# Inputs of the first stage laid out beforehand, and one column group of TensorE for each modulation tile

## The chip, the cores and the metric

The kernel runs on one core of one Trainium2 chip. The metric is the device time of one execution in microseconds (us). Times are told as the median of several executions; the rows come from one more execution that the hardware profiler recorded.

## The reference, cut to what matters

Two transformer blocks run one behind the other on 512 tokens of 1024 channels, in float32. The change lies in the first stage of the first block, and in two smaller inputs of it:

```python
c_act = jax.nn.silu(c)                                   # c: (1, 1024)
cond = c_act @ ada_w[i] + ada_b[i]                       # ada_w: (1024, 6 * 1024)
shift1, scale1, gate1, shift2, scale2, gate2 = jnp.split(cond, N_MOD, axis=-1)
h = modulate(rmsnorm(x, norm1_g[i]), shift1, scale1)     # h * (1 + scale) + shift
z = h @ w_in[i] + b_in[i]                                # w_in: (1024, 2048)
u, v, val, gate = jnp.split(z, [D_A, 2 * D_A, 2 * D_A + D_B], axis=-1)
...
w = jnp.where(causal[None], w_s, jnp.zeros_like(w_s))    # w_s: (8, 128, 128)
mixed = jnp.einsum('hts,bcshd->bcthd', w, v) + b_s ...
```

The rest is a causal convolution of width 31 on val * sigmoid(gate), an output projection, a gated feed-forward layer, an attention block with three branches, a pooling block and two more feed-forward layers.

## The kernel before, in words

Activations stand with channels on partitions: `Xp` holds x as four tiles of two channel blocks by 512 tokens, `H` holds the modulated h as eight tiles of a high and a low part (`hx.t[k][:, 0]` and `[:, 1]`). Every product of the model is done in three float32r matmuls (high by high, high by low, low by high), so each weight slab that arrives (`raw`, 512 KB) is split by ScalarE into a high part `wh` and by VectorE into a low part `wl`; the class `Weights` (`W`) loads slabs in the planned order and splits them, and `W.ahead(n)` makes sure that n are split.

The first stage runs from the start to the last product of the "wave". Its parts, in the order in which the program gives them:

- `load_vecs` brings small vectors as rows (tile `rows`), and its `turn` transposes them on TensorE into columns. `turn_c` does this for c, `turn_1` for the norm gain and the modulation bias; `turn_2`, `turn_3` and `turn_4` come later.
- x arrives with tokens on partitions (four tiles `xtok`). ScalarE squares each half of a tile and sums it along the way (`accum_out`), a square root and a reciprocal give `rsc`, 32 transposes turn x into `Xp`, and `spread` makes a row of reciprocals on all partitions with four matmuls.
- `piece(q)`, q = 0 to 3, computes two channel blocks of shift1 and two of scale1: `ada_cols` multiplies the 32-fold copy `c32` of silu(c) with two slabs of `ada_w` at a time. Four column groups of 32 columns of the array each take one block of input channels and 256 output columns; the four partial sums are transposed and added by VectorE (`tensor_reduce`).
- `front(q)` makes two tiles of H from `Xp`, the row of reciprocals, and the modulation.
- `products(q)` does 24 matmuls with these two tiles, for four output tiles that stay open over all q (`wave`). With `WV = (6, 0)` and `WT = 4`, 6 products run, then the 16 matmuls of `piece(q + 1)`, then 4 products, then the transposes of the piece, `front(q + 1)`, and the other 14 products.

In this stage the instructions of VectorE, ScalarE and TensorE stand in program order (`ordered(True)`); the DMA queue of SyncE and everything behind the stage is ordered by the compiler's planner. The planner also decides which tile takes which place in SBUF, so a load can wait for the last reader of the tile that stood in its place. A float32 matmul (not float32r) is two instructions of TensorE in the trace.

Behind the wave comes the convolution (taps on VectorE and GpSimd), the v projection, the spatial mixing, whose weights `wsr` are masked by GpSimd and transposed in eight matmuls into `wsT`, and `turn_4`. All helpers issue on one line, so the profile shows L113 for nearly all compute; the tiles tell them apart. L218 is `load_vecs`, L237 loads x, L249 is `ada_load`, L309 is `W.load`.

Of the kernel before, what the change touches and what calls it, by code (L numbers as in the profile page):

```python
# [22 lines left out]
KF0 = 14  # L23
KT0 = 16
LD = 2
WV = (6, 0)
WT = 4
DEEP = 2
DEEPF = 1
# [1 line left out]
HS = 256  # L31
# [50 lines left out]
PS3 = 1  # L82


TAGS = {}
TAGSETS = 0
B1 = ("cv", "glu", "bvs", "wsr", "wsT", "vt", "uT")
NB1 = 11
WW = ()
NBW = 20  # L90
TAGS.update({n: ("b1", NB1) for n in B1})
# [29 lines left out]
def body(ctx: ExitStack, tc: tile.TileContext, I: dict, out, dbg=None):  # L121
    nc = tc.nc
    cp = ctx.enter_context(tc.tile_pool(name="cp", bufs=1))
# [5 lines left out]
    V, G, SC, TE = (Ordered(tc, e) for e in (nc.vector, nc.gpsimd, nc.scalar, nc.tensor))  # L129
# [11 lines left out]
    def SQ():  # L141
        return tp.tile([P, S], F32, tag="sq", name="sq", bufs=BS)
# [27 lines left out]
    def stt(o, a, s, b, op0, op1):  # L170
        return V.scalar_tensor_tensor(o, a, s, b, op0=op0, op1=op1)
# [36 lines left out]
    def flat(apx):
        n = len(apx.shape)
        letters = "abcde"[:n]  # L210
        return apx.rearrange(f"{' '.join(letters)} -> ({' '.join(letters)})") if n > 1 else apx

    def load_vecs(gi, grp, eng=nc.sync):

        rt = rows.rearrange("p a (s c) -> p (a s) c", c=P)[:, gi]
        r0 = 0
        for name, src, n in grp:
            eng.dma_start(rt[r0:r0 + n, :P], flat(src).rearrange("(r p) -> r p", p=P))  # L218
            r0 += n

        def turn():
            pt = ST()
            TE.transpose(pt[:, :r0], rt[:r0, :P], ident[:r0, :r0])
            col = C(r0)
            V.tensor_copy(col, pt[:, :r0])
            c0 = 0
            for name, src, n in grp:
                vecs[name] = col[:, c0:c0 + n]
                c0 += n
        return turn  # L230

    rows = A("rows")
    turn_c = load_vecs(0, [("c", I["c"], 8)])
    xt = []
    for i in range(4):
        a = A("xtok")
        nc.sync.dma_start(a, I["x"][0, i * P:(i + 1) * P, :].rearrange("p (j c) -> p j c", j=2))  # L237
        xt.append(a)
    turn_1 = load_vecs(1, [("norm1", I["norm1_g"], 8), ("adab", I["ada_b"], 48), ("b_in", I["b_in"], 16)], nc.scalar)
# [36 lines left out]
    Xp = [cp.tile([P, 2, S], F32, name=f"X{q}") for q in range(4)]  # L276

    def x_(k, c0=0, c1=S):
        return Xp[k // 2][:, k % 2, c0:c1]

    H = [cp.tile([P, 2, S], F32R, name=f"H{k}") for k in range(KD)]

# [61 lines left out]
    def plan_cols(w, k0, kt, c0, n):  # L344
        W.plan([(0, P, 0, n, rows_of(w, k0, kt, c0, n))], kt, n)

    w_in = I["w_in"][0]
    for c in range(4):
        W.pool = c < WP
        W.hp = HP  # L350
        plan_cols(w_in, 0, 8, 1024 + c * P, P)
        plan_cols(w_in, 0, 8, 1536 + c * P, P)
    for b in range(4):
        plan_cols(w_in, 2 * b, 2, 512, S)
    for c in range(4):
        plan_cols(w_in, 0, 8, c * P, P)
    for k0 in (0, 4):
        for g in range(4):
            plan_cols(I["w_out"][0], k0, 4, g * HS, HS)
# [185 lines left out]

    adaw = []
    for q in range(4):
        if q < 2:
            W.load()
            W.load()  # L550
        adaw.append([ada_load(ada, c0 + HS * q, HS) for c0 in (0, D)])
    turn_2 = load_vecs(2, [("cw", I["b_conv_w"], 124)])
    turn_3 = load_vecs(3, [("norm2", I["norm2_g"], 8), ("normf", I["norm_f_g"], 8), ("conv_b", I["b_conv_b"], 4), ("gn_g", I["b_gn_g"], 4),
                           ("gn_b", I["b_gn_b"], 4), ("ona", I["out_norm_a_g"], 4), ("onb", I["out_norm_b_g"], 4), ("lng", I["a_ln_g"], 4),
                           ("lnb", I["a_ln_b"], 4), ("psc", I["pool_scale_2"], 8), ("adafb", I["ada_f_b"], 16), ("pe", I["nsa_cmp_pe_2"], 32)])

    ordered(True)
    turn_c()
    act(cact, vecs["c"], AF.Silu)
    V.tensor_copy(c32, cact.unsqueeze(2).to_broadcast([P, KD, 32]))  # L560
    ssx = C(8).rearrange("p (a b) -> p a b", a=4)
    rsc = C(4)
    for i in range(4):
        for j in range(2):
            act(SQ(), xt[i][:, j], AF.Square, accum_out=ssx[:, i, j:j + 1])
    V.tensor_reduce(rsc, ssx, axis=AX.X, op=OP.add)
    act(rsc, rsc, AF.Sqrt, scale=1.0 / D, bias=epsc)
    V.reciprocal(rsc, rsc)
    for k in range(KD):
        pt = AXP()  # L570
        for i in range(4):
            TE.transpose(pt[:, i * P:(i + 1) * P], xt[i][:, k // 4, (k % 4) * P:(k % 4 + 1) * P], ident)
        V.tensor_copy(x_(k), pt)
    rsx = ACC()
    act(rsx, spread(rsc, S), AF.Copy)
    W.ahead(2)
    turn_1()
    adab = vecs["adab"]

# [191 lines left out]
    for q in range(4):  # L771
        w = products(q)
        if q < 3:
            pc = piece(q + 1)
            for n in WV:
                for _ in range(n):
                    next(w)
                for _ in range(8):
                    next(pc)
            for _ in range(WT):  # L780
                next(w)
            drain(pc)
            front(q + 1)
# [952 lines left out]
```

## Time and profile before

| | |
|---|---|
| runs | median of 3: 1685.77 us (1684.52 to 1688.46) |
| profiled execution | 1689.51 us, its span 1687.8 us |
| TensorE busy | 1651.7 us, 98% of the span |
| VectorE, ScalarE, GpSimd busy | 857.5, 686.3, 130.1 us |
| granted TensorE clock, mean | 0.991 |

The span runs from the first to the last instruction; 1.7 us of the profiled execution lie outside it. A granted clock of 1.00 is 2.4 GHz and 0.50 is 1.2 GHz. Busy time of TensorE is modelled at its end, so a busy TensorE isn't one at its peak.

### The profile page before, as it was taken

To read this page: it belongs to the slowest core of one execution; us is meant where nothing else is said; L and a number is where in the kernel's file an instruction comes from. 1 tells how busy PE (TensorE), PEld (TensorE's weight loads), DVE (VectorE), ACT (ScalarE), POOL (GpSimd) and SP (SyncE) were. 2 spreads that over 40 slices of the span, in tenths; PEclk is the share of its full clock that TensorE was granted. 3 is DMA by queue.
4 is the path that set the end of the run, shared out by engine and by line. 5 is a ranking of instruction groups with operands and counts; after the bars stand their busy time and mean duration, and the time that the engine had idled before them with its cause. 6 is when DMAs were issued, how large, how long until landed. Compare 5 with 4: busy or idle time off the path is not lost.

```text
span 1687.8 us, 22593 instructions
## 1 busy us (share of the span) xinstructions
PE 1651.7 (98%) x9033; PEld 1370.7 (81%) x9033; DVE 857.5 (51%) x1636; ACT 686.3 (41%) x1246; POOL 130.1 (8%) x144
## 2 busy tenths in 40 slices
PE   7998999999999999999999999999998999999998
PEld 4885798777888998877768988888887998888886
DVE  5798672333333485678776434433248744341244
ACT  4685452232222364446558422223237832222222
POOL 0452000000000002100002000000012100000002
PEclk8998999999999999999999999999999999999999
DMA  9636544455331424311125223234321432232511
GB/s 302 177 117 197 181 114 129 148 165 164 89 103 57 113 61 94 89 38 37 40 72 147 70 80 96 88 113 121 92 87 51 133 98 70 76 114 98 150 38 50
DMA packets 263602, 179.58 MB, mean 106 GB/s; under 512 B 20688, under 2 KB 244800, under 8 KB 263496
## 3 DMA queue, kind: packets, MB, share of 16 engines
q1 hardware_dynamic: 258952, 176.99, 36.0%
q10 hardware_dynamic: 4544, 1.14, 0.4%
q8 instruction: 71, 1.16, 0.3%
q14 instruction: 35, 0.29, 0.1%
HBM read 175.99 MB, written 2.11 MB: 106 GB/s over the span
## 4 chain that ended last, share of the span: by engine, by line
PE 93%; DVE 3%; ACT 2%; DMA 2%; SPq 1%; issue 0%; DVEq 0%; ACTq 0%
PE mm L113 84%; PE ax L113 4%; PE st L113 4%; DMA raw<-in_w_ffn_in_dram 1%; DMA adaw<-in_ada_w_dram 0%; SPq L249 0%; DMA raw<-in_w_out_dram 0%; ACT sq L113 0%; DVE wl L113 0%; ACT pw L113 0%; DVE pw L113 0%; DVE ax L113 0%; DVE XT L113 0%; ACT wh L113 0%; ACT H L113 0%
## 5 line engine op out<-in xcount | busy, mean ns | idle before, releaser
L113 PE MATMUL mm<-H,wh 128*128 128x512 f32 (+1 forms) x3168 | 872.8, 361 | 2.2 <-ACT H L113 2.2
L113 PEld LDWEIGHTS mm<-H,wh 128*128 128x128 f32 x3168 | 563.5, 189 | 99.1 <-issue 9.1
L113 PE MATMUL mm<-H,wl 128*128 128x512 f32 (+1 forms) x1584 | 568.5, 359 | 0.0
L113 DVE TENSOR_TENSOR wl<-raw,wh 128x1024 fp32r<-128x1024 f32 (+1 forms) x257 | 311.8, 1226 | 281.4 <-ACT wh L113 262.7
L113 PEld LDWEIGHTS mm<-H,wl 128*128 128x128 f32 x1584 | 299.9, 189 | 44.4 <-issue 1.0
L113 ACT ACTIVATE wh<-raw 128x1024 fp32r<-128x1024 f32 (+1 forms) x257 | 262.2, 1041 | 146.0 <-PE mm L113 89.5
L113 PE MATMUL mm<-wh,hid 128*128 128x512 f32 x704 | 217.3, 389 | 0.0
L113 DVE TENSOR_TENSOR silu<-silu,mm 128x512 f32<-128x512 f32 (+1 forms) x77 | 47.0, 611 | 256.9 <-PE mm L113 252.9
L113 PEld LDWEIGHTS mm<-wh,hid 128*128 128x128 f32 x704 | 132.1, 188 | 27.2
L113 ACT ACTIVATE hid<-silu 128x512 fp32r<-128x512 f32 (+1 forms) x77 | 43.9, 570 | 268.0 <-DVE silu L113 268.0
L113 PE MATMUL mm<-wl,hid 128*128 128x512 f32 x352 | 137.3, 390 | 0.0
L113 PE MATMUL mm<-hid,wh 128*128 128x512 f32 (+1 forms) x464 | 116.6, 340 | 0.0
L113 PEld LDWEIGHTS mm<-hid,wh 128*128 128x128 f32 x464 | 80.2, 190 | 10.0 <-issue 0.4
L113 POOL TENSOR_TENSOR mg<-mg,gb 128x512 f32<-128x512 f32 x32 | 44.4, 1395 | 467.7 <-ACT sq L113 424.3
L113 ACT ACTIVATE silu<-silu 128x512 f32<-128x512 f32 (+1 forms) x52 | 29.3, 565 | 124.4 <-DVE silu L113 124.3
L113 PE MATMUL mm<-hid,wl 128*128 128x512 f32 (+1 forms) x232 | 79.0, 340 | 0.0
L113 PEld LDWEIGHTS mm<-wl,hid 128*128 128x128 f32 x352 | 66.1, 188 | 14.0 <-DVE wl L113 0.3
L113 DVE TENSOR_TENSOR silu<-mm,rsb 128x512 f32<-128x512 f32 (+1 forms) x52 | 31.6, 608 | 73.7 <-PE mm L113 73.2
L113 DVE TENSOR_TENSOR hid<-silu,hid 128x512 fp32r<-128x512 f32 (+1 forms) x77 | 47.3, 615 | 36.9 <-ACT hid L113 36.8
L113 PE MATMUL mm<-wh,H 128*128 128x512 f32 (+2 forms) x256 | 65.4, 344 | 0.2 <-ACT H L113 0.2
L113 POOL TENSOR_TENSOR cv<-cv,tap 128x488 f32<-128x488 f32 (+12 forms) x40 | 53.5, 1370 | 91.6 <-ACT cv L113 71.3
L113 ACT ACTIVATE silu<-mm 128x512 f32<-128x512 f32 (+1 forms) x25 | 13.6, 546 | 95.4 <-PE mm L113 95.4
(263 smaller groups left out, 1648.5 us busy)
## 6 DMA issues: line engine op xcount, KB each, us to landing
adaw<-in_ada_w_dram SPq DMA_DIRECT2D x48, 512.0 KB
raw<-in_w_ffn_in_dram SPq DMA_DIRECT2D x44, 512.0 KB
raw<-in_ffn_w_gate_dram SPq DMA_DIRECT2D x44, 512.0 KB
raw<-in_ffn_w_up_dram SPq DMA_DIRECT2D x44, 512.0 KB
raw<-in_ffn_w_down_dram SPq DMA_DIRECT2D x44, 512.0 KB
raw<-in_w_in_dram SPq DMA_DIRECT2D x16, 512.0 KB
adaw<-in_ada_f_w_dram SPq DMA_DIRECT2D x16, 512.0 KB
raw<-in_attn_w_in_dram SPq DMA_DIRECT2D x16, 512.0 KB
```

The source lines that it names most:

```text
L113: ins = f(*a, **k)
```

## The change

x, the vectors, the modulation weights of the first two parts, the input projection and the spatial weights are put in other orders of the same numbers before the launch (`laid_out`), so that each partition reads one contiguous run: 4 KB for x, for a slab of modulation weights, for a slab of w_in and for the spatial weights. In the kernel the transposes of x, of the vectors and of the spatial weights are gone. The sums of squares of x, which now run across partitions, are made by TensorE: for each of eight channel blocks ScalarE squares the block and four float32 matmuls with a column of ones add it up. In `piece`, a column group of 32 columns now computes one of the four 128-wide output blocks over all eight channel blocks, so nothing is left to add behind it; it is 32 matmuls of 128 columns in place of 16 of 256, one transpose in place of four. The modulation weights of q = 0 are loaded ahead of the first two weight slabs, and the split of these slabs moves from ahead of `piece(0)` into `front(0)`. `WV` becomes (20, 8, 8): the number of products ahead of the piece, for each q.

```diff
-WV = (6, 0)
+WV = (20, 8, 8)
-B1 = ("cv", "glu", "bvs", "wsr", "wsT", "vt", "uT")
-NB1 = 11
+B1 = ("cv", "glu", "bvs", "wsT", "vt", "uT")
+NB1 = 10
...
-    rows = A("rows")
-    turn_c = load_vecs(0, [("c", I["c"], 8)])
-    xt = []
-    for i in range(4):
-        a = A("xtok")
-        nc.sync.dma_start(a, I["x"][0, i * P:(i + 1) * P, :].rearrange("p (j c) -> p j c", j=2))
-        xt.append(a)
-    turn_1 = load_vecs(1, [("norm1", ...), ("adab", ...), ("b_in", ...)], nc.scalar)
+    def load_vecs(src, names, eng):
+        n = sum(w for _, w in names)
+        col = C(n)
+        eng.dma_start(col, I[src])
+        c0 = 0
+        for name, w in names:
+            vecs[name] = col[:, c0:c0 + w]
+            c0 += w
...
+    load_vecs("va", VA, nc.scalar)
+    for q in range(4):
+        nc.sync.dma_start(Xp[q], I["xt"][q])
...
+    def plan_win(c):
+        W.plan([(0, P, 0, P, I["w_in_p"][c].rearrange("p (k m) -> p k m", k=8))], 8, P)
...
     for q in range(4):
+        sl = [A("adaw") for _ in range(4)]
+        for a, src in zip(sl, I["ada_p"][q]):
+            nc.sync.dma_start(a, src)
+        adaw.append(sl)
         if q < 2:
             W.load()
             W.load()
-        adaw.append([ada_load(ada, c0 + HS * q, HS) for c0 in (0, D)])
-    turn_2 = load_vecs(2, ...)
-    turn_3 = load_vecs(3, ...)
+    load_vecs("vb", VB, nc.sync)
...
-    for i in range(4):
-        for j in range(2):
-            act(SQ(), xt[i][:, j], AF.Square, accum_out=ssx[:, i, j:j + 1])
-    V.tensor_reduce(rsc, ssx, axis=AX.X, op=OP.add)
-    act(rsc, rsc, AF.Sqrt, scale=1.0 / D, bias=epsc)
+    pst = ST()
+    for k in range(KD):
+        q = SQ()
+        act(q, x_(k), AF.Square)
+        for i in range(4):
+            TE.matmul(pst[:, i:i + 1], lhsT=q[:, i * P:(i + 1) * P], rhs=ones[:, 0:1], start=(k == 0 and i == 0), stop=(k == KD - 1 and i == 3))
+    act(rsc, pst[:, :4], AF.Sqrt, scale=1.0 / D, bias=epsc)
     V.reciprocal(rsc, rsc)
-    for k in range(KD):
-        pt = AXP()
-        for i in range(4):
-            TE.transpose(pt[:, i * P:(i + 1) * P], xt[i][:, k // 4, (k % 4) * P:(k % 4 + 1) * P], ident)
-        V.tensor_copy(x_(k), pt)
-    rsx = ACC()
-    act(rsx, spread(rsc, S), AF.Copy)
-    W.ahead(2)
-    turn_1()
+    rsp = spread(rsc, S)
+    rsx = ACC()
...
     def piece(q):
-        g = [ada_cols(adaw[q][x], 8 * x + 2 * q, adab[...], AXP) for x in range(2)]
...
+        pq = AXP()
+        for k in range(KD):
+            for j in range(4):
+                yield TE.matmul(pq[32 * j:32 * j + 32, :P], lhsT=c32[:, k, :], rhs=adaw[q][k // 2][:, k % 2, j * P:(j + 1) * P],
+                                start=(k == 0), stop=(k == KD - 1))
+        sb = T("adasb")
+        act(sb[:, :P], pq[:, :P], AF.Copy)
+        pt = AXP()
+        yield TE.transpose(pt[:, :P], sb[:, :P], ident)
+        for x in range(2):
+            ks = slice(8 * x + 2 * q, 8 * x + 2 * q + 2)
+            tt(mod[:, ks], pt[:, :P].rearrange("p (j r) -> p j r", j=4)[:, 2 * x:2 * x + 2, 0], adab[:, ks], OP.add)
...
-    def front(q):
+    def front(q, rs, between=None):
...
-                stt(t, x_(k), g1[:, k:k + 1], rsx, OP.mult, OP.mult)
+                stt(t, x_(k), g1[:, k:k + 1], rs, OP.mult, OP.mult)
...
+            if k == 2 * q + 1 and between is not None:
+                between()
...
-    front(0)
+    front(0, rsp, lambda: W.ahead(2))
+    act(rsx, rsp, AF.Copy)
...
-            for n in WV:
-                for _ in range(n):
-                    next(w)
-                for _ in range(8):
-                    next(pc)
+            for _ in range(WV[q]):
+                next(w)
+            for _ in range(32):
+                next(pc)
...
-    turn_2()
-    turn_3()
...
-    wsr = A("wsr")
     wsT = A("wsT")
-    nc.sync.dma_start(wsr.rearrange(...), I["a_spatial_w"][0].rearrange("h t s -> t h s"))
-    G.affine_select(wsr, wsr, pattern=[[0, 8], [-1, P]], ...)
-    turn_4 = load_vecs(4, [("ng2", I["norm_g_2"], 64)])
+    nc.sync.dma_start(wsT, I["wst"])
+    G.affine_select(wsT, wsT, pattern=[[0, 8], [1, P]], ...)
...
-    for b in range(2):
-        pt = ST()
-        for h in range(4):
-            TE.transpose(pt[:, h * P:(h + 1) * P], wsr[:, b, h * P:(h + 1) * P], ident)
-        act(wsT[:, b], pt, AF.Copy)
-    turn_4()
...
+def laid_out(a):
+    import numpy as np
+    a = {k: np.asarray(v) for k, v in a.items()}
+    for name, group in (("va", VA), ("vb", VB)):
+        a[name] = np.concatenate([a[SOURCE[v]].reshape(w, P).T for v, w in group], axis=1)
+    a["xt"] = a["x"][0].T.reshape(4, 2, P, S).transpose(0, 2, 1, 3)
+    p = a["ada_w"][0][:, :2 * D].reshape(4, 2, P, 2, 4, 2, P)
+    a["ada_p"] = p.transpose(4, 0, 2, 1, 3, 5, 6).reshape(4, 4, P, 2, S)
+    a["w_in_p"] = a["w_in"][0].reshape(KD, P, 16, P).transpose(2, 1, 0, 3).reshape(16, P, D)
+    a["wst"] = a["a_spatial_w"][0].transpose(2, 0, 1).reshape(P, 2, S)
+    return a
```

The loads of the w_in slabs for val, gate and u go through `plan_win`; the four slabs for v stay as they were. `VA` and `VB` list the vectors with their numbers of columns: 80 columns for c, the norm gain, the modulation bias and the input bias, 288 for the others.

## Rows read from the trace of the kernel before

**Rows 1.** The page: the chain that ended last, share of the span by engine.

```profile
PE 93%; DVE 3%; ACT 2%; DMA 2%; SPq 1%; issue 0%; DVEq 0%; ACTq 0%
```

**Rows 2.** Timeline of TensorE, first stage: start, us taken, operation, count, [idle before].

```profile
19.24 0.96 PE L113 MATMUL ax<-adaw,fixed 128*32 128x256 f32 x8 [0.85 <-DMA adaw<-in_ada_w_dram]
...
23.62 1.58 PE L113 MATMUL mm<-H,wh 128*128 128x512 f32 x2 [2.19 <-ACT H L113]
...
26.84 3.30 PE L113 MATMUL ax<-adaw,fixed 128*32 128x256 f32 x32
...
36.21 1.93 PE L113 MATMUL ax<-adaw,fixed 128*32 128x256 f32 x32
```

**Rows 3.** The chain that ended last, in order of time: start, us.

```profile
47.70 8.65 PE mm L113 x38
```

**Rows 4.** Timeline of ScalarE, first stage.

```profile
4.92 0.63 ACT L113 ACTIVATE sq<-xtok 128x512 f32<-128x512 f32 x1 [1.19 <-DMA xtok<-in_x_dram]
...
12.32 0.30 ACT L113 ACTIVATE fixed<-fixed 128x4 f32<-128x4 f32 x1
...
15.93 1.99 ACT L113 ACTIVATE wh<-raw 128x1024 fp32r<-128x1024 f32 x2
...
20.31 0.38 ACT L113 ACTIVATE adasb<-ax 128x256 f32<-128x256 f32 x1 [2.11 <-PE ax L113]
...
22.85 1.39 ACT L113 ACTIVATE H<-t,fixed 128x512 fp32r<-128x512 f32 x2 [2.16 <-DVE t L113]
```

**Rows 5.** Timeline of VectorE, first stage and around 136 us.

```profile
12.65 0.18 DVE L113 RECIPROCAL fixed<-fixed 128x4 f32<-128x4 f32 x1 [1.45 <-ACT fixed L113]
...
17.51 2.35 DVE L113 TENSOR_TENSOR wl<-raw,wh 128x1024 fp32r<-128x1024 f32 x2
...
23.60 1.41 DVE L113 SCALAR_TENSOR_TENSOR H<-t,fixed,H 128x512 fp32r<-128x512 f32 x2
...
136.69 1.22 DVE L113 TENSOR_TENSOR wl<-raw,wh 128x1024 fp32r<-128x1024 f32 x1 [1.39 <-ACT wh L113]
```

**Rows 6.** Timeline of SyncE's DMA queue: issue time, time taken, load, count.

```profile
0.80 0.40 SPq L218 DMA_DIRECT2D rows<-in_c_dram  x1
1.26 1.78 SPq L237 DMA_DIRECT2D xtok<-in_x_dram  x4
...
101.71 25.14 SPq L249 DMA_DIRECT2D adaw<-in_ada_w_dram  x12
```

**Rows 7.** Stretches: busy time (x instructions) by engine, granted clock, DMA share, GB/s.

```profile
4.00:8.00 4.00, 0.95 (x2) 0.36 (x2) 0.05 (x1) 2.67 (x8) 0.00 (x0) 1.00 0.99 372
...
9.60:12.60 3.00, 2.97 (x14) 2.97 (x15) 0.17 (x1) 2.90 (x6) 0.00 (x0) 1.00 1.15 302
...
23.60:29.60 6.00, 5.98 (x34) 3.16 (x38) 3.77 (x4) 2.91 (x4) 0.00 (x0) 0.50 1.09 348
...
695.30:698.60 3.30, 3.30 (x9) 2.55 (x9) 2.70 (x11) 0.35 (x1) 0.00 (x0) 0.50 1.08 341
```

**Rows 8.** Timeline of TensorE, later stages.

```profile
99.98 1.04 PE L113 MATMUL st<-fixed,wsr 128*128 128x128 f32 x8
...
130.12 3.77 PE L113 MATMUL mm<-wsT,vt 128*64 128x128 f32 x64
...
141.85 3.64 PE L113 MATMUL mm<-adaw,fixed 128*32 128x256 f32 x32 [5.02 <-DVE sp L113]
...
153.62 0.95 PE L113 MATMUL st<-fixed,acc 128*128 128x1 f32 x8
156.31 2.04 PE L113 MATMUL st<-fixed,rs 128*128 128x128 f32 x8 [1.75 <-DVE rs L113]
...
691.67 3.64 PE L113 MATMUL ax<-fixedR,nq 128*128 128x32 f32 x32
```

**Rows 9.** Weight loads by shape (count, busy us, mean ns), 23.6:29.6, then 36:56.

```profile
L113 PEld LDWEIGHTS mm<-H,wh 128*128 128x128 f32 x4 | 1.2, 309 | 3.3 <-ACT H L113 2.6 <-DVE H L113 0.5
...
L113 PEld LDWEIGHTS mm<-H,wh 128*128 128x128 f32 x44 | 8.1, 188 | 2.4 <-ACT adasb L113 0.8
```

More of the change, by code (lines that the diff above doesn't have):

```diff
@@ L82 @@
 PS3 = 1
+VA = (("c", 8), ("norm1", 8), ("adab", 48), ("b_in", 16))
+VB = (("cw", 124), ("norm2", 8), ("normf", 8), ("conv_b", 4), ("gn_g", 4), ("gn_b", 4), ("ona", 4), ("onb", 4), ("lng", 4), ("lnb", 4),
+      ("psc", 8), ("adafb", 16), ("pe", 32), ("ng2", 64))
+SOURCE = {"c": "c", "norm1": "norm1_g", "adab": "ada_b", "b_in": "b_in", "cw": "b_conv_w", "norm2": "norm2_g", "normf": "norm_f_g",
+          "conv_b": "b_conv_b", "gn_g": "b_gn_g", "gn_b": "b_gn_b", "ona": "out_norm_a_g", "onb": "out_norm_b_g", "lng": "a_ln_g",
+          "lnb": "a_ln_b", "psc": "pool_scale_2", "adafb": "ada_f_b", "pe": "nsa_cmp_pe_2", "ng2": "norm_g_2"}
 TAGS = {}
 TAGSETS = 0
-B1 = ("cv", "glu", "bvs", "wsr", "wsT", "vt", "uT")
-NB1 = 11
+B1 = ("cv", "glu", "bvs", "wsT", "vt", "uT")
+NB1 = 10
 WW = ()
@@ L206, in body, with x_ @@
     vecs = {}
[L208 to L221, printed above, removed]
-            pt = ST()
[L223 to L230, printed above, removed]
-    rows = A("rows")
-    turn_c = load_vecs(0, [("c", I["c"], 8)])
-    xt = []
-    for i in range(4):
-        a = A("xtok")
-        nc.sync.dma_start(a, I["x"][0, i * P:(i + 1) * P, :].rearrange("p (j c) -> p j c", j=2))
-        xt.append(a)
-    turn_1 = load_vecs(1, [("norm1", I["norm1_g"], 8), ("adab", I["ada_b"], 48), ("b_in", I["b_in"], 16)], nc.scalar)
+    def load_vecs(src, names, eng):
[6 more added lines that the diff above has]
+            c0 += w
+    Xp = [cp.tile([P, 2, S], F32, name=f"X{q}") for q in range(4)]
+    def x_(k, c0=0, c1=S):
+        return Xp[k // 2][:, k % 2, c0:c1]
+    load_vecs("va", VA, nc.scalar)
+    for q in range(4):
+        nc.sync.dma_start(Xp[q], I["xt"][q])
     ada = I["ada_w"][0]
@@ L274, in ada_cols @@
         tt(mod[:, col:col + n], rd[:, :n], bias, OP.add)
-    Xp = [cp.tile([P, 2, S], F32, name=f"X{q}") for q in range(4)]
-    def x_(k, c0=0, c1=S):
-        return Xp[k // 2][:, k % 2, c0:c1]
     H = [cp.tile([P, 2, S], F32R, name=f"H{k}") for k in range(KD)]
@@ L350, in body @@
         W.hp = HP
-        plan_cols(w_in, 0, 8, 1024 + c * P, P)
-        plan_cols(w_in, 0, 8, 1536 + c * P, P)
+        plan_win(8 + c)
+        plan_win(12 + c)
     for b in range(4):
@@ L355, in body @@
     for c in range(4):
-        plan_cols(w_in, 0, 8, c * P, P)
+        plan_win(c)
     for k0 in (0, 4):
@@ L550, in body @@
             W.load()
-        adaw.append([ada_load(ada, c0 + HS * q, HS) for c0 in (0, D)])
[L552 to L555, printed above, removed]
+    load_vecs("vb", VB, nc.sync)
@@ L557, in body @@
     ordered(True)
-    turn_c()
     act(cact, vecs["c"], AF.Silu)
     V.tensor_copy(c32, cact.unsqueeze(2).to_broadcast([P, KD, 32]))
-    ssx = C(8).rearrange("p (a b) -> p a b", a=4)
     rsc = C(4)
-    for i in range(4):
-        for j in range(2):
-            act(SQ(), xt[i][:, j], AF.Square, accum_out=ssx[:, i, j:j + 1])
-    V.tensor_reduce(rsc, ssx, axis=AX.X, op=OP.add)
-    act(rsc, rsc, AF.Sqrt, scale=1.0 / D, bias=epsc)
-    V.reciprocal(rsc, rsc)
-    for k in range(KD):
-        pt = AXP()
-        for i in range(4):
-            TE.transpose(pt[:, i * P:(i + 1) * P], xt[i][:, k // 4, (k % 4) * P:(k % 4 + 1) * P], ident)
-        V.tensor_copy(x_(k), pt)
+    pst = ST()
@@ L574, in body @@
+    for k in range(KD):
[4 more added lines that the diff above has]
+    act(rsc, pst[:, :4], AF.Sqrt, scale=1.0 / D, bias=epsc)
+    V.reciprocal(rsc, rsc)
+    rsp = spread(rsc, S)
     rsx = ACC()
-    act(rsx, spread(rsc, S), AF.Copy)
-    W.ahead(2)
-    turn_1()
     adab = vecs["adab"]
     def piece(q):
-        g = [ada_cols(adaw[q][x], 8 * x + 2 * q, adab[:, 8 * x + 2 * q:8 * x + 2 * q + 2], AXP) for x in range(2)]
-        for x in g:
-            for _ in range(8):
-                yield next(x)
-        for x in g:
-            yield from x
+        pq = AXP()
[10 more added lines that the diff above has]
+            tt(mod[:, ks], pt[:, :P].rearrange("p (j r) -> p j r", j=4)[:, 2 * x:2 * x + 2, 0], adab[:, ks], OP.add)
@@ L774, in body @@
             pc = piece(q + 1)
-            for n in WV:
-                for _ in range(n):
-                    next(w)
-                for _ in range(8):
-                    next(pc)
+            for _ in range(WV[q]):
+                next(w)
+            for _ in range(32):
+                next(pc)
             for _ in range(WT):
@@ L782, in body @@
             drain(pc)
-            front(q + 1)
+            front(q + 1, rsx)
         drain(w)
@@ L800, in body @@
         nc.sync.dma_start(bs[64 * e:64 * e + 64], I["a_spatial_b"][0].rearrange("(h e) t -> e h t", e=2)[e:e + 1].to_broadcast([64, 4, P]))
-    wsr = A("wsr")
     wsT = A("wsT")
-    nc.sync.dma_start(wsr.rearrange("p a (h s) -> p (a h) s", h=4), I["a_spatial_w"][0].rearrange("h t s -> t h s"))
-    G.affine_select(wsr, wsr, pattern=[[0, 8], [-1, P]], compare_op=OP.is_ge, fill=0.0, base=0, channel_multiplier=1)
-    turn_4 = load_vecs(4, [("ng2", I["norm_g_2"], 64)])
+    nc.sync.dma_start(wsT, I["wst"])
+    G.affine_select(wsT, wsT, pattern=[[0, 8], [1, P]], compare_op=OP.is_ge, fill=0.0, base=0, channel_multiplier=-1)
     pump(PU[0], PP[0])
@@ L837, in body @@
     tt(nmu, nmu, vrs, OP.mult)
-    for b in range(2):
-        pt = ST()
-        for h in range(4):
-            TE.transpose(pt[:, h * P:(h + 1) * P], wsr[:, b, h * P:(h + 1) * P], ident)
-        act(wsT[:, b], pt, AF.Copy)
-    turn_4()
     pr = ST()
@@ L1726 @@
     arrays, args = {}, {}
-    for name, a in inputs.items():
+    for name, a in laid_out(inputs).items():
         a = np.ascontiguousarray(a)
```

## The prediction

> **What bounds the kernel now.** I read the page first. By its chain of waits TensorE alone holds 93% of the span [rows 1], and its busy time is 98%. So a gain has to take TensorE time away, or a hole in it. Next I read the timeline of TensorE in the first stage. The reader is to see that it works in pieces until 23.62 and without a hole behind it: the last slab of piece 0 lands just before 19.24, and the first product of the wave starts at 23.62 behind the first tile of H [rows 2]. The chain in order of time then holds matmuls only, to 56.35, where the wave ends [rows 3]. The later holes are few; the largest is 5.02 us ahead of 141.85 [rows 8].
>
> Third I read the granted clock, since TensorE idles early. From 23.6 to 29.6 it is 0.50, 1.2 GHz [rows 7]. For 9.6 to 12.6 the same column says 1.00, but 14 transposes took 2.97 us there, 0.212 each, and eight like them at 99.98 take 1.04 us, 0.13 each with their tail [rows 7, 8]. I trust the durations: the kernel begins at the half clock.
>
> **The change, part by part.** Times are those of the profiled execution.
>
> *Removed.* The transposes of x and the first two vector transposes ran while piece 0 was on its way; they are worth nothing, the cover being the DMA until 19.24 [rows 2]. Ahead of the later products go eight transposes of the spatial weights, 1.04 with their tail [rows 8], and three of vectors, about 0.1 each at that pace: 1.2 us of TensorE without a hole, taken in full.
>
> *Earlier data.* Before, the last slab of piece 0 stood behind x and two weight slabs, 5.2 MB; now behind x alone, 4.2 MB. The 5.2 MB took from 1.26 to 19.24 [rows 2, 6]; at that mean 4.2 MB need 14.4 us and have landed at 15.2, and sooner if the 4 KB runs go like x at 372 GB/s [rows 7]. That is 4.0 us earlier. It counts only if TensorE is there.
>
> *Added: the sums of squares on TensorE.* 8 blocks by 4 matmuls by 2 instructions make 64 instructions, each with a 128-column weight load for one column of data, in program order ahead of the spread and of piece 0. The trace has this shape later: eight in 0.95 us, 0.119 each; 32 with 32 columns of data take 3.64, 0.114 each [rows 8]. The width does not matter, so the load sets the pace. At the full clock 64 cost 7.6 us at most. At the half clock no such row exists. The bounds are 0.114 (a load that doesn't care) and 0.255 (the spread at 156.31, eight in 2.04 with the tail [rows 8]). The load of 128 columns takes 309 ns in the stretch at the half clock and 188 in the one at full [rows 9], so it does care; I take 0.212, the pace of the transposes [rows 7]. The Trainium skill, TensorE: Matmul & The Clock Gate, LDWEIGHTS (loading the stationary operand), prices a load at its columns over 1.2 in ns, 107 for 128 columns, at either clock. By that estimate the 64 take 6.8 us and rival 1 comes out. The trace agrees at the full clock and not at the half.
>
> Would the sums themselves bring the full clock? Behind the 32 narrow matmuls, in which TensorE was never idle, the clock fell to 0.50 from 695.3 to 698.6 [rows 7, 8]. So I expect not.
>
> x is issued at 0.80 in place of 1.26 [rows 6], so the first square starts near 4.5 and ends at 5.1 (0.63 [rows 4]). Squares come faster than sums, so the sums run through: 5.1 + 64 x 0.212 = 18.7. Square root 0.30 and reciprocal 0.18 with their hand-overs [rows 4, 5]: 19.2. The spread is eight instructions at 0.212: 20.9.
>
> *Piece 0.* 64 instructions of 128 columns in place of 32 of 256. 32 took 1.93 us at full clock, 0.060 each [rows 2]. Bounds: 0.030 (four groups side by side, paced by the data) and 0.060 (an instruction costs the same at any width). The nearest row, two groups of 64 columns on 128 of data, gives 3.77 / 64 = 0.059 [rows 8]: the same weight columns times data width as in the old piece, so half of it for the new shape. I take 0.030: a piece keeps its 1.93, and 3.5 at the half clock (32 took 3.30 there [rows 2]). Piece 0 ends at 24.4; before at 20.2.
>
> *The way to the first product.* Before, 20.2 to 23.62, 3.4 us. One transpose and no reduction save about 0.5: the first H is ready at 27.3. But the weights are now split behind it: the second H (0.70) and a wh of 1.0 [rows 4] put the first product at 29.0, 5.4 us later than before. Behind the split on ScalarE waits the copy of the reciprocals, and on VectorE two wl of 1.18 and the low part of the second H, 0.71 [rows 5]; the eighth of the first 12 products waits for it until 32.2. From there to the twentieth are 13 products: 3.0 us at 0.228 (38 in 8.65 [rows 3]), 5.6 at half. The last split is ready at 34.6 and is used in between, so the twentieth ends at 35.5 to 37.8.
>
> *Piece 1 and a new wait.* 1.93 (3.5 at half), then 4 products, 0.9. All 24 products of q = 0 are then used up, so `front(1)` stands bare: 3.4 less the saved 0.5 and the copy of 0.38 that hides behind the four products [rows 4], 2.5 us. The wave goes on at 40.8 to 44.7. It still has 72 products (16.4), two pieces (3.9) and two transposes (0.3); 12 products, 2.7 us, cover each later front. End: 61.4 to 65.3, before 56.35. I take 62.6, a little under the middle, since by then TensorE has been busy for long: a loss of 6.3 us.
>
> *Behind the stage.* At 136.69 VectorE had waited 1.39 for a split whose slab came late, and 5.02 of TensorE hang on its order [rows 5, 8]. The tile `rows`, read last by a transpose near 101.4, lay where the first of 12 loads had to go at 101.71 [rows 6]. Without it loads can start earlier. Bounds: 5.0 gained, or nothing; the planner may also place work worse. VectorE works up to that wait, so I take 0.5. The 4 KB runs of later slabs lie under TensorE without holes: nothing.
>
> *Sum.* 6.3 - 1.2 - 0.5 = 4.6. The profiled execution took 1689.5 with a span of 1687.8, 3.7 above the median of the runs, so I set the sum on the median: 1685.8 + 4.6 = 1690.4. What a measurement of this kernel tells from no change is 0.2%, 3.4 us.
>
> **The rivals.**
>
> 1. *The sums hide.* TensorE has the full clock during them, or the loads are indifferent to it. Sums end at 5.1 + 7.6 = 12.7, the spread at 14.2 (eight at 0.12 and 0.5 ahead), piece 0 near 16.3, the first H at 19.2, the first product at 20.9. The fourth weight slab, another 4.2 MB at 372 GB/s, lands near 26.4; its wh and wl put the twentieth product at 29.1. With 1.93 + 0.9 + 2.5 and 20.6 the wave ends at 55.0, 1.3 earlier. With 1.7 from behind the stage: 1682.8. It decides when the 64 sums take under 9 us or so. For it: the transposes ran at the full clock later. Against it: [rows 7 to 9] as above.
> 2. *An instruction has a floor.* Each narrow matmul costs 0.060, whatever its width. The four pieces then cost 1.93 more each, piece 0 twice that at half clock: 9.6 us, 1700. Against it: 64 x 128 and 32 x 256 fit one price per area. For it: no row read here is under 0.059 on the average. The Trainium skill, TensorEngine Tiling (Array Packing), Instruction Overhead, gives each matmul about 60 cycles and warns against tiling what is already small. By that estimate (0.025 to 0.050 by the clock) the piece would lie at its old time or up to 1.3 us above.
> 3. *The late hole closes.* The first stage loses as forecast, but earlier loads take the 5.02 at 141.85 away: 1690.4 - 4.5 = 1685.9. For it: that hole hangs on one load. Against it: VectorE had only 1.39 of idle time there.
> 4. *The bare front lets the clock fall.* Behind a hole of 1.75 us the eight instructions at 156.31 ran at twice their time [rows 8]. A fall behind the hole of 2.5 costs some 1.7 us more: 1692.
>
> **How the numbers follow.** Forecast with rival 4 inside it 0.64, rival 1 0.17, rival 2 0.10, rival 3 0.09. The forecast's own range is 1687 to 1695: the ends of the stage at 61.4 and 65.3 lose 5.0 to 9.0, 1.2 to 2.5 come off behind it, rival 4's 1.7 may come on top, and the hand-overs are uncertain by 1. To leave out 2 in 10 the range takes in rival 1 and part of rival 2: 1682 to 1698. Slower by over 0.2% (above 1689.1) comes from three quarters of the forecast and from nearly all of rival 2; faster (under 1682.4) from less than half of rival 1 and from a better plan behind the stage than I count on. Slower 0.57, same 0.31, faster 0.12.
>
> **What would show it.** Right: 64 instructions of one column in some 13 us, the reciprocals only near 19, the first product near 29, a hole of 2 to 3 us behind piece 1, the wave's end past 60. Wrong: the sums over by 13; a piece of over 3 us at the full clock (rival 2); no hole ahead of the output projection's part of the modulation (rival 3). The forecast falls above all with the early clock.

## The result, and the profile after

The changed kernel takes 1708.22 us in the median of 6 runs, the kernel before 1686.96 beside it: a ratio of 1.0131, 95% interval 1.0117 to 1.0144. It is slower by about 22 us. The forecast was slower by 4.6, so the sign held and the size did not: 1708 lies 10 us above the range. The first profiled execution of the changed kernel took 1848.9 us at a granted clock of 0.85 throughout and is left out of the ratio; the profile shown here is a second one of the same kernel (1709.49 us, span 1707.8).

The page, the chain that ended last, beside [rows 1]:

```profile
PE 89%; DVE 3%; ACT 3%; DMA 2%; issue 1%; POOL 1%; SPq 0%; DVEq 0%; ACTq 0%; POOLq 0%
```

The chain in order of time (start, us), first stage, beside [rows 2, 3]:

```profile
5.46 13.83 PE st L119 x64
19.94 2.05 PE st L119 x8
21.98 3.62 PE ax L119 x64
...
29.99 1.22 PE mm L119 x2
31.25 6.65 PE mm L119 x18
37.90 1.89 PE ax L119 x64
39.79 1.12 PE mm L119 x4
...
43.08 3.84 PE mm L119 x8
...
57.92 8.39 PE mm L119 x36
```

The reader finds the forecast step by step: 64 sums, the spread, piece 0, the first product at 29.99, piece 1, and between 41.0 and 43.08 the bare `front(1)`. The wave ends at 57.92 + 8.39 = 66.3, before at 56.35 [rows 3]. That is 10.0 of the 20.0 us by which the two spans differ. The other ten are lost behind it. TensorE's timeline there (a hole ahead of a row, with its releaser, in brackets), beside [rows 8]:

```profile
90.46 0.50 PE L119 MATMUL mm<-wl,H 128*128 128x512 f32 x1 [0.59 <-DVE wl L119]
...
120.52 1.98 PE L119 MATMUL st<-cv,fixed 128*128 128x512 f32 x4 [1.02 <-DVE cv L119]
...
153.66 1.94 PE L119 MATMUL mm<-adaw,fixed 128*32 128x256 f32 x16 [4.85 <-DVE sp L119]
158.68 0.69 PE L119 MATMUL st<-fixed,adasb 128*128 128x128 f32 x2 [3.09 <-ACT adasb L119]
...
205.41 1.08 PE L119 MATMUL mm<-adaw,fixed 128*32 128x256 f32 x8 [1.27 <-DMA adaw<-in_ada_w_dram]
```

Stretches of the changed kernel (busy time of TensorE, its weight loads, VectorE, ScalarE, GpSimd; then the granted clock):

```profile
5.40:19.40 14.00, 13.82 (x64) 13.73 (x64) 0.68 (x3) 5.45 (x10) 0.00 (x0) 1.00 0.91 368
...
43.00:46.40 3.40, 3.32 (x7) 2.35 (x8) 1.41 (x2) 0.69 (x2) 0.00 (x0) 0.50 0.01 2
152.20:162.40 10.20, 5.65 (x36) 2.38 (x40) 9.18 (x16) 7.07 (x13) 2.69 (x3) 0.50 0.32 104
203.40:210.20 6.80, 5.48 (x29) 3.26 (x30) 2.04 (x6) 2.92 (x4) 0.00 (x0) 0.50 0.91 284
220.50:223.90 3.40, 2.98 (x10) 2.62 (x11) 3.40 (x8) 2.27 (x5) 0.00 (x0) 0.50 0.00 0
```

and the only stretches at the half clock between 130 and 230 us in the kernel before:

```profile
138.90:145.70 6.80, 3.85 (x34) 1.66 (x34) 6.80 (x9) 5.55 (x12) 3.13 (x3) 0.50 0.00 0
156.00:159.30 3.30, 2.99 (x17) 1.98 (x17) 2.35 (x6) 0.60 (x1) 0.00 (x0) 0.50 1.01 334
```

So 10.1 us at the half clock have become 20.4. One trace of each kernel doesn't carry this far: the second trace of the kernel before (e11) has 6.8 us there, and the two traces of the mended kernel below (e5, e12), which are one program, have 20.3 and 10.1. Marks of the traces in us (the modulation begins with the first `mm<-adaw` behind the wave; the last mark is the first `mm<-hid,wh`):

| kernel | wave ends | modulation begins | between these two | `mm<-hid,wh` | between the last two | span |
|---|---|---|---|---|---|---|
| before | 56.35 | 134.03 | 77.7 | 407.25 | 273.2 | 1687.8 |
| before, second trace (e11) | 54.95 | 132.64 | 77.7 | 404.05 | 271.4 | 1687.5 |
| changed (e0) | 66.30 | 144.44 | 78.1 | 427.14 | 282.7 | 1707.8 |
| e1 | 61.98 | 141.79 | 79.8 | 422.42 | 280.6 | 1701.7 |
| e2 | 64.23 | 139.50 | 75.3 | 420.96 | 281.5 | 1703.9 |
| e6 | 61.43 | 139.60 | 78.2 | 422.53 | 282.9 | 1702.2 |
| e4 | 66.24 | 148.43 | 82.2 | 430.78 | 282.4 | 1711.3 |
| e5, mended first stage | 56.70 | 131.93 | 75.2 | 412.12 | 280.2 | 1692.9 |
| e5, second trace (e12) | 56.76 | 132.03 | 75.3 | 407.39 | 275.4 | 1691.1 |
| e10, mended, late part undone | 56.98 | 136.03 | 79.1 | 407.52 | 271.5 | 1688.2 |

Of the 10 us behind the wave 9.5 fall between the last two marks (between the modulation's start and `mm<-hid,wh`). The holes over 0.35 us there are 4.85 + 3.09 + 0.39 + 0.50 + 1.27 + 1.18 + 0.89 = 12.2, before 5.02 + 1.75 + 0.50 + 1.00 + 0.48 = 8.75: 3.4 more. Another 10.3 us at the half clock, in which TensorE does half its work, are up to 5.2. Together they are up to 8.6 of the 9.5.

### The profile page after: what moved, and what is told of

It is laid out like the page before. It is cut to its first block, busy times and chain, and to the rows that moved or that the text cites. A ratio compares the mean times of both kernels' runs of the same rounds, so it can differ in the third digit from the quotient of the medians.

```text
span 1847.2 us, 22801 instructions
## 1 busy us (share of the span) xinstructions
PE 1810.7 (98%) x9168; PEld 1427.0 (77%) x9168; DVE 852.5 (46%) x1614; ACT 684.9 (37%) x1233; POOL 127.2 (7%) x144
## 3 DMA queue, kind: packets, MB, share of 16 engines
q8 instruction: 72, 1.18, 0.3%
## 4 chain that ended last, share of the span: by engine, by line
PE 94%; DVE 2%; DMA 2%; ACT 1%; issue 0%; SPq 0%; DVEq 0%; ACTq 0%
PE mm L119 85%; PE st L119 5%; PE ax L119 4%; DMA adaw<-in_ada_w_dram 1%; DMA raw<-in_w_ffn_in_dram 0%; DMA raw<-in_w_out_dram 0%; DVE ax L119 0%; DVE wl L119 0%; DVE H L119 0%; ACT H L119 0%; ACT wh L119 0%; DMA raw<-in_ffn_w_up_dram 0%; DMA fixed<-in_va_dram 0%; ACT sq L119 0%; DVE mg L119 0%
## 5 line engine op out<-in xcount | busy, mean ns | idle before, releaser
L119 PE MATMUL mm<-H,wh 128*128 128x512 f32 (+1 forms) x3168 | 935.9, 383 | 6.4 <-ACT wh L119 3.7
L119 PEld LDWEIGHTS mm<-H,wh 128*128 128x128 f32 x3168 | 580.5, 195 | 144.6 <-issue 10.3
L119 PE MATMUL mm<-H,wl 128*128 128x512 f32 (+1 forms) x1584 | 604.9, 382 | 0.0
L119 PEld LDWEIGHTS mm<-H,wl 128*128 128x128 f32 x1584 | 308.9, 195 | 67.9 <-issue 2.8
L119 PE MATMUL mm<-wh,hid 128*128 128x512 f32 x704 | 235.5, 417 | 0.0
L119 PE MATMUL mm<-wl,hid 128*128 128x512 f32 x352 | 146.9, 417 | 0.0
L119 PE MATMUL mm<-hid,wh 128*128 128x512 f32 (+1 forms) x464 | 124.7, 358 | 0.0
L119 PEld LDWEIGHTS mm<-wl,hid 128*128 128x128 f32 x352 | 67.7, 192 | 20.9
L119 PE MATMUL mm<-hid,wl 128*128 128x512 f32 (+1 forms) x232 | 83.7, 361 | 0.0
L119 PE MATMUL mm<-wh,H 128*128 128x512 f32 (+2 forms) x256 | 69.9, 362 | 0.5 <-ACT H L119 0.2
```

The source lines that it names most:

```text
L119: ins = f(*a, **k)
```

## The experiments

Gains and losses below are (ratio - 1) times the median of the kernel before on the same chip, so the changed kernel stands at +22.1 (20 to 24). The medians of the kernel before beside the runs lie between 1685.3 and 1687.0.

**e0, the changed kernel again**, without an edit: the profile above.

> The changed kernel once more, unedited, for a profile of it without disturbance. Theory A (the sums of squares at the half clock and the bare front lose 6 us in the first stage, and something behind the stage loses the rest): the wave ends near 62 us (before 56.35), and another 13 to 16 us are lost between there and 230 us. Rival B (the first stage loses nearly all of it): the wave ends past 72 us.

Neither case came out: the wave ends at 66.3, and 10 us are lost behind it.

**e1, sums on VectorE.**

```
-        for i in range(4):
-            TE.matmul(pst[:, i:i + 1], lhsT=q[:, i * P:(i + 1) * P], rhs=ones[:, 0:1], start=(k == 0 and i == 0), stop=(k == KD - 1 and i == 3))
+        if k:
+            tt(sacc, sacc, q, OP.add)
+    for i in range(4):
+        TE.matmul(pst[:, i:i + 1], lhsT=sacc[:, i * P:(i + 1) * P], rhs=ones[:, 0:1], start=(i == 0), stop=(i == 3))
```

> The eight squared blocks are added up on VectorE, and TensorE makes 4 sums in place of 32 (8 instructions in place of 64). Theory A: the sums end near 14 us in place of 19.5, the first product starts near 24.5 in place of 30.2, and the whole kernel gets 5 to 6 us faster than the changed one, to about 1702. If the sums were hidden by the landing of piece 0: no difference. Theory C (the time is lost by the order that the planner makes behind the stage, which any edit moves): a difference of another size, either sign.

Measured: 1702.69, ratio 1.0095 (1.0078 to 1.0112), +16.0. TensorE's timeline of e1:

```profile
14.53 1.87 PE L119 MATMUL st<-fixed,acc 128*128 128x1 f32 x8 [14.53 <-DVE acc L119]
...
27.06 1.22 PE L119 MATMUL mm<-H,wh 128*128 128x512 f32 x2 [3.65 <-ACT wh L119]
```

The sums end at 16.4 (expected 14), the first product comes 2.9 us earlier (expected 5.7), the wave ends 4.3 earlier, and the kernel gains some 6.

**e2, the first split ahead of piece 0.**

```
+    W.ahead(2)
     pc = piece(0)
     drain(pc)
-    front(0, rsp, lambda: W.ahead(2))
+    front(0, rsp)
```

> The split of the first two weight slabs stands ahead of piece 0 again, as before the change, in place of between the tiles of H in the first front. Theory A: the first product starts behind the first H, near 28.3 in place of 30.2, and the first 12 products don't wait for the splits; 2 to 4 us faster than the changed kernel, about 1705. If the split is hidden: no difference. Theory C: a difference of another size, either sign.

Measured: 1701.54, ratio 1.0089 (1.007 to 1.0108), +15.0. The wave ends only 2.1 earlier, but the modulation begins 4.9 earlier. Behind the wave the holes of 0.59 and 1.02 are gone. ScalarE's timeline shows why, first of the changed kernel, then of e2:

```profile
72.17 1.87 ACT L119 ACTIVATE tap<-glu,fixed 128x486 f32<-128x486 f32 x3
75.22 0.71 ACT L119 ACTIVATE tap<-glu,fixed 128x485 f32<-128x485 f32 x1 [1.18 <-POOL cv L119]
...
78.23 0.70 ACT L119 ACTIVATE tap<-glu,fixed 128x483 f32<-128x483 f32 x1 [0.29 <-POOL cv L119]
78.83 1.04 ACT L119 ACTIVATE wh<-raw 128x1024 fp32r<-128x1024 f32 x1
```

```profile
70.18 4.23 ACT L119 ACTIVATE tap<-glu,fixed 128x486 f32<-128x486 f32 x7
74.32 1.04 ACT L119 ACTIVATE wh<-raw 128x1024 fp32r<-128x1024 f32 x1
```

The same seven taps stand ahead of the same split in both. In e2 they run through; in the changed kernel four wait for GpSimd to have read an earlier tap, and `wh` with its `wl` comes 2.4 us later after the wave's end (12.5 against 10.1). The edit touches neither taps nor GpSimd, and behind the first stage the order of instructions on every engine is the same. What differs is what they wait for: by the semaphores of the traces, 120 of the 342 loads issued after 60 us wait for other engines in e2 than in the changed kernel, as many in e5, 6 in e6 and 14 in e1, where the split stays, and none between two traces of one program. With the order the same, that points to which tiles share a buffer.

The kernel before has such waits too, 0.69 + 0.30 + 0.31 + 0.78 = 2.1 us in all. The first and the last of them:

```profile
65.26 0.70 ACT L113 ACTIVATE tap<-glu,fixed 128x484 f32<-128x484 f32 x1 [0.69 <-POOL cv L113]
...
71.45 0.70 ACT L113 ACTIVATE tap<-glu,fixed 128x482 f32<-128x482 f32 x1 [0.78 <-POOL cv L113]
```

So e2 and e5, at 75.3 us between the wave and the modulation, are 2.4 quicker there than the kernel before, and the changed kernel, at 78.1, is only 0.4 slower: these waits are hardly a part of what the change lost.

**e3 and e4, the late part alone, and undone.** From here the expectations set two theories against each other: A, the loss behind the stage comes from the order that the planner gives the modulation; B, it follows from the late first stage. e3 is the kernel before with `wsT` loaded as `wst`, no transposes and NB1 10; e4 the changed kernel with

```
-    nc.sync.dma_start(wsT, I["wst"])
+    wsr = A("wsr")
+    nc.sync.dma_start(wsr.rearrange("p a (h s) -> p (a h) s", h=4), I["a_spatial_w"][0].rearrange("h t s -> t h s"))
...
+            TE.transpose(pt[:, h * P:(h + 1) * P], wsr[:, b, h * P:(h + 1) * P], ident)
```

> The kernel before with one late part of the change alone: the spatial weights come laid out (`wst`), so the eight transposes and the tile `wsr` are gone and NB1 is 10; the first stage, the vectors and the layouts of x, w_in and ada_w stay as before. Theory A, the loss behind the first stage comes from the order that the planner chooses for the modulation's matmuls and copies once this part has changed: to 100 us the trace is that of before, 1.0 us is saved on the transposes, and then TensorE waits more than before between 130 and 230 us; 1690 to 1695 us. Theory B, the loss behind is a consequence of the late and slow first stage (loads and clock): 1684.5 to 1686, one us saved and no new hole.

> The changed kernel with that late part undone: `wsr` is loaded as before, transposed eight times by TensorE, NB1 is 11. Theory A: the order behind the stage is again near that of before, so that most of the 9 us behind it come back, less 1 for the transposes: 1700 to 1702 us. Theory B: the first stage is as late as in the changed kernel, so nothing comes back and the transposes are added: 1709 to 1711 us.

Measured: e3 1690.93, ratio 1.003 (1.0015 to 1.0046), +5.1, where TensorE had 1.0 us less to do: A's side. e4 1704.33, ratio 1.0125 (1.0099 to 1.0152), +21.1, not to be told from the changed kernel: A's 7 to 9 us did not come back, though the median lies below B's range too. In e4's trace TensorE waits for `adaw` between 204 and 211 in three holes, 4.2 us in all; the changed kernel has one there, of 1.27. In e3's trace the order is another (the hole of 5.02 is 1.56, and behind it stand 2.03 and 0.78 for `adasb`), but that execution was the quickest of six, and where the 5 us of the others lie it doesn't show; its modulation stretch takes 275.7, 2.5 and 4.3 more than the two of before.

**e5, the first stage mended**: e1 and e2 together, and `WV = (8, 8, 8)` in place of `(20, 8, 8)`. **e6, the last of the three alone.**

> The changed kernel with three edits of the first stage at once: squares added on VectorE (4 matmuls in place of 32), the first weight split ahead of piece 0, and piece 1 behind 8 products in place of 20, so that 16 products lie behind front(1). The first two alone gave back 4.3 and 2.1 us by the end of the wave; the third takes away the hole of 2.1 behind piece 1 and the fall of the clock behind it, some 3.3. So the wave should end within 1 us of before's 56.35. Theory A, the loss behind the stage has its own cause: 8 to 9 us remain and the kernel takes 1694 to 1697 us. Theory B, that loss follows from the late first stage: the kernel is as fast as before or faster, 1683 to 1687 us.

> The changed kernel with piece 1 behind 8 products in place of 20, nothing else, so that 16 products lie behind the last transpose of piece 1 and cover front(1). If the bare front costs what the trace of the changed kernel shows, its hole of 2.06 us and the half clock behind it (3.4 us at half pace, 1.7 lost) go away: the wave ends near 62.5 in place of 66.3, and the kernel takes 1703 to 1705 us. If the time behind the first product is set by the late weight splits instead, the hole moves ahead into the first 12 products and 1707 to 1709 stay.

Measured: e5 1689.99, ratio 1.0023 (1.0011 to 1.0034), +3.9; e6 1703.47, ratio 1.0118 (1.01 to 1.0135), +19.9. Chain in time of e6, then TensorE's timeline of e5:

```profile
33.81 2.32 PE ax L119 x64
36.13 1.12 PE mm L119 x4
37.37 4.74 PE mm L119 x20
...
53.07 8.38 PE mm L119 x36
```

```profile
25.41 0.50 PE L119 MATMUL mm<-H,wh 128*128 128x512 f32 x1 [2.05 <-ACT H L119]
...
29.37 1.96 PE L119 MATMUL ax<-adaw,fixed 128*32 128x128 f32 x64
...
141.39 1.94 PE L119 MATMUL mm<-adaw,fixed 128*32 128x256 f32 x16 [5.09 <-DVE sp L119]
146.41 0.69 PE L119 MATMUL st<-fixed,adasb 128*128 128x128 f32 x2 [3.08 <-ACT adasb L119]
```

In e6 the hole behind piece 1 and the half clock after it are gone, and the wave ends at 61.4, 4.9 earlier; it was the bare front, as e6's first case had it, though by the ratios the time fell by 2.2 only (by the medians 4.7; each interval reaches 2 to 3 us to either side). In e5 the wave ends at 56.7, level with the first trace of before, and 18 of the 22 us are back, twice what the wave's end gives; the time lies between the ranges of the two theories. Yet on every engine the order of instructions behind the first stage is that of the changed kernel, instruction by instruction; so order can't be the cause of what e5 regained there. The wave's end gives 9.6 of it and the way to the modulation 2.9, as in e2; the stretch behind gives 2.5 in one trace and 7.3 in the other. The holes of 5.1 and 3.1 are in both traces of e5. What is not in them is the wait for `adaw` at 205. SyncE's queue, changed kernel, then e5:

```profile
165.19 0.92 SPq L241 DMA_DIRECT2D adaw<-in_ada_w_dram  x2
166.15 0.51 SPq L296 DMA_DIRECT2D raw<-in_w_out_dram  x1
166.70 4.68 SPq L241 DMA_DIRECT2D adaw<-in_ada_w_dram  x4
184.89 0.37 SPq L296 DMA_DIRECT2D raw<-in_w_out_dram  x1
```

```profile
163.97 3.33 SPq L241 DMA_DIRECT2D adaw<-in_ada_w_dram  x2
167.40 1.36 SPq L296 DMA_DIRECT2D raw<-in_w_out_dram  x1
168.86 2.79 SPq L241 DMA_DIRECT2D adaw<-in_ada_w_dram  x2
171.75 1.35 SPq L296 DMA_DIRECT2D raw<-in_w_out_dram  x1
```

In the changed kernel the queue stands from 171.4 to 184.9, with 6 of this stretch's `adaw` loads issued; e5 has issued 12 by 176. Its waits from 150 to 212 (us, times, longest) name TensorE as the one that had to free the buffer:

```profile
SPq L296 <- PE st L119: 13.7, 2, 13.5
```

The list of loads is the same; what each waits for is not. But the stand of 13.5 us is not what makes the stretch long: e2's queue doesn't stand there (four `adaw`, a `raw` and two more `adaw` loads go from 165.0 to 175.7), its loads wait for the same engines as e5's (one of 340 differs), and its stretch still takes 281.5.

**e7 and e8, another order of the modulation**, on the changed kernel and on e5: ScalarE's order is held and three pieces stand between the gate's four blocks.

```
+            for _ in range(between[hp]):
+                ada_step(1)
...
+    SC.on = True
-    spatial(0, S)
+    spatial(0, S, (0, 1, 2, 0))
+    SC.on = False
-    for _ in range(NA[0]):
+    for _ in range(NA[0] - 3):
```

> The changed kernel, its first stage unedited, with three of the six modulation pieces emitted between the four blocks of the spatial gate, and ScalarE's work of that stretch kept in the order of the program, so that the copies `adasb` stand ahead of the third block's H as they did before. Theory A (order): the hole of 3.09 ahead of the first transposes of `adasb` falls under 1 us and the stretch at the half clock gets shorter: 3 to 6 us back, 1702 to 1705 us. Theory B (the late first stage sets it): the stretch waits for something else as late, 1707 to 1709 us.

> The kernel with the mended first stage and the same edit of the modulation's order. Theory A: 3 to 6 us less than 1690.0, that is 1684 to 1687, no slower than before. Theory B: nothing left to gain, 1689 to 1691 us.

**e9, other banks for the modulation**, on e5: `ada_step(1, AXP)` in place of `ada_step(1)`.

> The kernel with the mended first stage, and the six modulation pieces behind the spatial gate in the two PSUM banks `ax` in place of the four `mm`, which the gate's own blocks hold until VectorE has read them. If the hole of 5.09 (which ends on VectorE's third `sp`) is only a wait for a bank, it goes away with the one of 3.08 and most of the 13.7 us at the half clock: 1680 to 1684 us, faster than before. If TensorE then waits as long for the first H and the first weights of the output projection, 1687 to 1691 us.

Measured: e7 1705.63, ratio 1.0125 (1.0108 to 1.0142), +21.1; e8 1692.16, ratio 1.0047 (1.0029 to 1.0065), +7.9; e9 1691.28, ratio 1.0044 (1.0026 to 1.0061), +7.4. TensorE's holes in e7:

```profile
156.46 0.69 PE L119 MATMUL st<-fixed,adasb 128*128 128x128 f32 x2 [5.65 <-ACT adasb L119]
160.90 1.94 PE L119 MATMUL mm<-adaw,fixed 128*32 128x256 f32 x16 [1.88 <-issue]
163.71 0.69 PE L119 MATMUL st<-fixed,adasb 128*128 128x128 f32 x2 [0.87 <-ACT adasb L119]
```

The two holes of 7.9 us together are three of 8.4, and e7's median lies between the ranges of the two theories. In e9 the wait for a bank is gone, and TensorE stands 3.08 us for the first H of the output projection and in six smaller holes behind it. So the misses of e8 and e9 point one way: at this place TensorE waits for VectorE's chain behind a late weight slab, and these orders only choose which instruction stands there. This is read from the timelines; no run brought the slab earlier. In the changed kernel ScalarE's timeline has that slab, as VectorE's had it in [rows 5]:

```profile
147.40 1.06 ACT L119 ACTIVATE wh<-raw 128x1024 fp32r<-128x1024 f32 x1 [1.71 <-DMA raw<-in_w_out_dram]
```

Theory A's price for ScalarE's order, 3 to 6 us, fell.

**e10, the mended first stage with the late part undone.**

> The kernel with the mended first stage and, besides, the late part undone (`wsr` transposed by TensorE, NB1 11). If first stage and late part add up: the late part alone cost some 5 us on the kernel before and its undoing gave 4 on the changed kernel, so 1690.0 - 4 to 5 = 1685 to 1686 us, level with before, the transposes of 1.0 included. If the gain of the mended first stage was already the whole of it: 1690 to 1691 us.

Measured: 1689.85, ratio 1.0023 (1.0008 to 1.0037), +3.9, as e5. The stretch of the modulation is as short as before's (271.5), but begins 4.1 us later than in e5: the two parts do not add up. TensorE's timeline has here another order of the modulation, and the second hole is nearly gone:

```profile
142.93 2.77 PE L119 MATMUL mm<-adaw,fixed 128*32 128x256 f32 x18 [4.10 <-DVE sp L119]
...
149.02 0.73 PE L119 MATMUL mm<-H,wh 128*128 128x512 f32 x2 [0.48 <-ACT adasb L119]
```

**e11 and e12, second traces** of the kernel before and of e5.

> The kernel before, unedited, for a second trace of it: its profiled execution lay 3.7 us above the median of its runs, the mended kernels stand 4 us above that median and yet end with it in the traces. If the part that varies is the half clock at the start of the wave, this trace ends near 1683 to 1685 with the wave over at 53 to 54, and the mended first stage is still 3 us behind it. If the part that varies lies behind the stage, the wave ends at 56 again and the stretch from 130 to 230 us is shorter by 3 to 5.

> The kernel with the mended first stage, unedited, for a second trace on the same chip: its first lay 4.6 us above its median. Wave end near 56.7 again; behind it, a hole of 3.1 ahead of the transposes of `adasb` again if that is the fixed order of the queues, and less than 20.5 us at the half clock between 130 and 230 if the clock is what varies from one execution to the next.

Measured: 1689.27 and 1692.86, one run each. The kernel before ends its wave at 54.95, 1.8 ahead of e12's, and its modulation stretch takes 4.0 less; between the two the mended kernel is 2.4 quicker (75.3 against 77.7). So 3.3 are left at `mm<-hid,wh`, out of both places. The holes of 5.2 and 3.1 are in e12 again, but of the 20.3 us that e5 has at the half clock between 130 and 230 only 10.1 are, as the last case of e12 had it: what lies at the half clock behind 190 in e5 is missing. Neither trace fell as low as 1685: e11 loses its 3 us again further on, between 689 and 730.

## Why the prediction was wrong

*Sums, spread, piece 0: right.* 64 instructions in 13.82 us, 0.216 each (forecast 0.212), the reciprocal over at 19.8 (19.2), the spread at 22.0 (20.9), piece 0 in 3.64 (3.5), the first product at 29.99 (29.0). The one us is the first square, 0.4 later, the sums, 0.2 longer, the hand-over ahead of the spread, and the spread itself, 2.05 in place of 1.7. The sums ran at half pace although the clock column shows 1.00 for them: before its first record the durations decide, as they did for [rows 7]. The Trainium skill, TensorE: Matmul & The Clock Gate, LDWEIGHTS (loading the stationary operand), gives 0.107 for such a load, with no term for the clock; the trace, at 0.216 for a load and its matmul, disagrees. The twentieth product ends at 37.9 (35.5 to 37.8), without the wait that was priced ahead of the eighth. *Rival 1 is out.*

*Piece: right.* 64 narrow instructions take 1.95 at the full clock, 0.030 each. *Rival 2 is out.*

*Piece 1 and the bare front: right in kind.* The hole is 2.06 (2.5), the wave goes on at 43.08 (40.8 to 44.7, 42.0 taken). *Rival 4 came true*: the clock is 0.50 from 43.0 to 46.4, and the eight products there take 3.84 where 1.82 were priced. The other 64 take 15.4 where 14.6 were priced. With 1.1 for the later start, and 0.2 less for pieces and transposes, these are the 3.7 us between 62.6 and 66.3: the term "6.3" measured 10.0. e6 shows that the front was bare, e1 what the sums cost.

*Behind the stage: the step that failed.* "Minus 1.2, minus 0.5" measured plus 10. The transposes did go. The load held by `rows` is issued earlier, at 87.86 in place of 101.71, but the other eleven begin at 123.35 in place of 110.94, and the hole stays at 4.85; *rival 3 is out*. The wrong step was to take the work behind the stage as the old work moved along. "The planner may also place work worse" stood among the bounds at nothing. The runs show in its place a modulation stretch of 282.7 us in place of 273.2, by 3.4 us more of holes and up to 5.2 from the half clock.

What of this is shown, and what is not:

- The hole of 3.09 ahead of `adasb` stands in e0, e1, e2, e5, e6 and e12, and in neither trace of before. It comes with the late part: with that undone on the mended kernel it is 0.48 and the stretch 271.5 (e10). But the kernel is no faster by it, and undone behind the late first stage the stretch stays at 282.4 (e4).
- The first stage changes what the instructions behind it wait for. e2 and e5 show it with all queues in the same order, and it is worth 2.9 us between the wave and the modulation. It doesn't explain the loss: the kernel before has such tap waits too and takes 77.7 us there against 78.1, and e2 has the waits of e5 with a stretch of 281.5.
- With the first stage mended 18 of 22 us come back, 9.6 by the wave's end and 2.9 up to the modulation. For the other 5.5 its two traces, of one program, give 2.5 and 7.3 in the stretch.

So the place of the loss is shown, and its cause only in part: how order, waits and clock share the 9.5 us stays open. That the sharing of buffers makes the waits is itself read from them; no run changed the sharing alone.

*Open.* What the mended kernel still lacks, 3.9 us (2 to 6). The late part costs 5.1 on the kernel before (e3), but nothing comes back when it is undone behind either first stage (e4, e10). No kernel tried beats the kernel before.

## What to carry to other kernels

Where a compiler gives out buffers and order for the whole kernel, an edit at its start is an edit of all of it: compare each queue's waits, not its order alone, before pricing what lies behind at nothing, and look whether the kernel before has the same waits before calling them the loss. Sums on a matmul with one column of data pay a full weight load each, here 0.216 us at the start of the kernel against 0.119 later; add up first on an engine that idles. Before a loop over pieces is widened, count what still covers the chain behind each piece.

## What the runs showed of the hardware

The price of a hole is more than the hole: behind the holes of some 5 and 3 us at the start of the modulation the clock was 0.50 for 13.6 us in e5 and for 10.1 in e12, the same program. Further on e5 has another 6.7 us at the half clock, behind holes of 0.39, 0.50 and 0.26 us; e12 has the same three holes and none. The stretches of e5, then the one of e12:

```profile
138.40:152.00 13.60, 7.53 (x51) 3.17 (x54) 12.45 (x19) 8.96 (x17) 4.21 (x4) 0.50 0.12 40
193.10:199.80 6.70, 6.44 (x34) 4.19 (x35) 2.18 (x7) 2.73 (x4) 0.00 (x0) 0.50 0.75 226
```

```profile
139.90:150.00 10.10, 5.32 (x32) 2.18 (x36) 9.15 (x16) 7.29 (x14) 2.91 (x3) 0.50 0.16 54
```

The clock differs from one execution of the same program to the next, and so do the marks: the two traces of the kernel before agree within 1.4 us at the wave's end, lie 3.2 apart at the first `mm<-hid,wh`, and end 0.3 apart, so that one trace of each kernel cannot settle 4 us.
